# Attention units two to a row: logits of two units together, transposes and values by twos between projection steps

## The chip, the cores and the metric

One core of a Trainium2 chip. The metric is the device time of one execution in microseconds (us), median of three runs. The engines are TensorE (PE in the profile; its weight loads are PEld), VectorE (DVE), ScalarE (ACT), GpSimd (POOL) and SyncE (SP), which here issues most DMAs.

## The reference, cut to what matters

A two-layer decoder trunk on 512 tokens of width 1024, float32: a Mamba-2 mixer and a convolutional FFN, then a shared key and value projection, differential attention, and a second FFN. The change lies in the attention of layer 1, for each block `i` of 128 queries:

```python
logits = jnp.einsum('bqhcd,bkhcd->bhcqk', qblk, k).astype(jnp.float32) * scale
logits = logits + bias[None, :, None]
logits = jnp.where(dist >= 0, logits, -jnp.inf)
p = jax.nn.softmax(logits, axis=-1)
attn = p[:, :, 0] - lam * p[:, :, 1]
return jnp.einsum('bhqk,bkhd->bqhd', attn.astype(v.dtype), v)
```

There are 8 heads, each with two maps (`c`) of depth 64 and values of width 128. Queries and keys are RMS-normed per head and map; the result is RMS-normed per head, scaled and projected back.

## The kernel before, in words

Large products run as three matmuls on a high and a low part of both operands (float32r). A weight chunk (512 KB) comes by a DMA on SyncE's queue (L139), ScalarE writes its high part (L165, or L147 without a gain), VectorE the low part (L166, L151). Chunks are split two ahead of use.

The attention stage works with two kinds of PSUM banks, four each: `mm` for projections and `aux` for everything else.

- **Projections** (`proj`, L924 to L946): a generator. One `next` is a *step*: two token blocks by two rows of weights by three matmuls (L932 to L934), 12 matmuls of 512 columns. Four chunks of two steps make one projection. The order is: keys and queries of heads 0 to 3, then, as filling between attention units, values 0 (`v0`), keys and queries of heads 4 to 7 (`k1`, `q1`), values 1 (`v1`), and the output projection of heads 0 to 3 (`attn_out`, whose steps have 6 matmuls).
- **Behind a key or query projection** (`qk`, L948): ScalarE copies (L954) and squares (L955), VectorE sums (L956), a root follows (`rsqrt_act`: L434 VectorE, L435 and L436 ScalarE, L437 to L439 VectorE), VectorE multiplies each of four blocks (L963), and the blocks are transposed on TensorE (L970, four transposes for each, into an `aux` bank) and copied out by ScalarE (L971). The transposes are put between two steps of the projection that follows.
- **A unit** (`Unit`, L985) is a part of a head: query blocks (0, 1), or (2), or (3), so 24 units with 384, 384 and 512 key columns. It has four actions.
  - `logits`: with a head's first part, the head's bias row is fetched (L1000, SyncE) and turned (L1001, VectorE). TensorE forms the logits of both maps (L1014, depth 64, the two maps in the two halves of the array) in two `aux` banks; VectorE adds the bias, writes to SBUF and takes the maximum (L1020), negates it (L1023); ScalarE takes the exponential and its sum (L1028).
  - `weigh`: VectorE, reciprocal of the sums (L1035), factor (L1037), difference of the maps (L1041).
  - `turn`: TensorE transposes the result (L1049) into an `aux` bank, ScalarE copies it out (L1050).
  - `values`: TensorE multiplies by the values (L1060, `aux`), ScalarE scales (L1063).
- After a head's last part `normed_out` (L1066: ScalarE L1070, VectorE L1071, the root, VectorE L1073) and, some units later, `turned_out` (L1075: transposes L1079, ScalarE L1082, VectorE L1083).

TensorE's order in this stage is the program's order, since the stage is built with a manual schedule for TensorE; the instructions of the other engines are ordered by the scheduler. The main loop (L1148 to L1167) takes one unit a turn: at turn `t`, transposes of unit `t-2`, logits of `t`, weights of `t-1`, values of `t-3`, and then the number of steps that the list `steps` (L1144) gives, two for the first 13 turns. Tile buffers: three for the logits of each map, two for the transposed result, four for the reciprocals.

Of the kernel before, what the change touches and what calls it, by code (L numbers as in the profile page):

```python
# [39 lines left out]
def trunk_kernel(ctx: ExitStack, tc, x, ssm_ln_g, ssm_in_w, ssm_conv_w, ssm_conv_b, ssm_dt_bias,  # L40
# [19 lines left out]
    def aux_bank(name):  # L60
        return pp.tile([P, T], F32, tag="aux", name=name)
# [368 lines left out]
    def rsqrt_act(v, pl, name, shape, n):  # L430

        m = pl.tile(shape, F32, tag="rs_m", name="rsm_" + name, bufs=2)
        t = pl.tile(shape, F32, tag="rs_t", name="rst_" + name, bufs=2)
        dve.tensor_scalar(out=m, in0=v, scalar1=1.0 / n, scalar2=EPS, op0=ALU.mult, op1=ALU.add)  # L434
        act.activation(v, m, AF.Ln)  # L435
        act.activation(v, v, AF.Exp, scale=-0.5)  # L436
        dve.tensor_tensor(out=t, in0=v, in1=v, op=ALU.mult)  # L437
        dve.scalar_tensor_tensor(out=t, in0=t, scalar=-0.5, in1=m, op0=ALU.mult, op1=ALU.mult)
        dve.scalar_tensor_tensor(out=v, in0=t, scalar=1.5, in1=v, op0=ALU.add, op1=ALU.mult)  # L439
# [18 lines left out]
    def run(gen):  # L458
        for _ in gen:
            pass  # L460
# [19 lines left out]
    def chain(*gens):  # L480
        for g in gens:
            yield from g
# [417 lines left out]
    with tc.tile_pool(name="att_o", bufs=1) as op_, tc.tile_pool(name="att", bufs=1) as ap:  # L900
# [47 lines left out]
        def qk(key, dst, gcol, where):  # L948
            kn, ss = [], ap.tile([P, NT, 8], F32, tag="qss", name="ss" + key, bufs=2)

            def evac(b, ps, rt):
                t = ap.tile([P, T], F32, tag="kn", name="kn%s_%d" % (key, b), bufs=4)
                s = ap.tile([P, T], F32, tag="ksq", name="ksq%s_%d" % (key, b), bufs=1)
                act.activation(t, ps, AF.Copy, scale=rt[:, b:b + 1])  # L954
                act.activation(s, t, AF.Square)  # L955
                dve.reduce_sum(ss[:, b, :], s.rearrange("p (a q) -> p a q", a=8), axis=AX.X)  # L956
                kn.append(t)

            yield from proj(key, evac)
            rsqrt_act(ss, ap, key, [P, NT, 8], 64)  # L960
            for b in range(NT):
                v = kn[b].rearrange("p (a q) -> p a q", a=8)
                dve.tensor_tensor(out=v, in0=v, in1=ss[:, b, :].unsqueeze(2).to_broadcast([P, 8, 64]),  # L963
                                  op=ALU.mult)

            def turned(bs):
                for b in bs:
                    ps = aux_bank("kt%s_%d" % (key, b))
                    for h in range(4):
                        pe.transpose(ps[:, h * P:(h + 1) * P], kn[b][:, h * P:(h + 1) * P], ident)  # L970
                    act.activation(dst[:, :, b * P:(b + 1) * P], ps.rearrange("p (h t) -> p h t", h=4),  # L971
                                   AF.Copy, scale=c2[:, gcol:gcol + 1])

            for at, bs in zip(where, ((0, 1), (2, 3))):
                late.append((at, lambda bs=bs: turned(bs)))

        def vproj(key, i):
            def evac(b, ps, rt):
                act.activation(vt[b][:, i * 512:(i + 1) * 512], ps, AF.Copy, scale=rt[:, b:b + 1])
            yield from proj(key, evac)  # L980

        PARTS = ((0, 1), (2,), (3,))
        fl = lambda a: a.rearrange("p a b -> p (a b)")

        class Unit:  # L985
# [66 lines left out]
            def values(self):  # L1052
                h = self.h
                if self.part == 0:
                    self.st["ot"] = ap.tile([P, NT, P], F32, tag="ot", name="ot%d" % h, bufs=2)
                ps = aux_bank("po" + self.tag)
                for j, i in enumerate(self.ii):
                    o = self.off[j]
                    for k in range(i + 1):
                        pe.matmul(ps[:, j * P:(j + 1) * P], self.at[:, o + k * P:o + (k + 1) * P],  # L1060
                                  vt[k][:, h * P:(h + 1) * P], start=(k == 0), stop=(k == i))
                for j, i in enumerate(self.ii):
                    act.activation(self.st["ot"][:, i, :], ps[:, j * P:(j + 1) * P], AF.Copy,  # L1063
                                   scale=self.rc[:, j, 0:1])

        def normed_out(h, st):  # L1066
            ot = st["ot"]
            sq = ap.tile([P, T], F32, tag="ksq", name="osq%d" % h, bufs=1)
            so = ap.tile([P, NT], F32, tag="so", name="so%d" % h, bufs=2)
            act.activation(sq, fl(ot), AF.Square)  # L1070
            dve.reduce_sum(so, sq.rearrange("p (a q) -> p a q", a=NT), axis=AX.X)  # L1071
            rsqrt_act(so, ap, "o%d" % h, [P, NT], P)
            dve.tensor_tensor(out=ot, in0=ot, in1=so.unsqueeze(2).to_broadcast([P, NT, P]), op=ALU.mult)  # L1073

        def turned_out(h, st):  # L1075
            ot = st["ot"]
            ps = aux_bank("oT%d" % h)
            for i in range(NT):
                pe.transpose(ps[:, i * P:(i + 1) * P], ot[:, i, :], ident)  # L1079
            oh_ = op_.tile([P, T], F32R, tag="oh", name="oh%d" % h, bufs=6)  # L1080
            ol_ = op_.tile([P, T], F32R, tag="ol", name="ol%d" % h, bufs=6)
            act.activation(oh_, ps, AF.Copy, scale=c2[:, 50:51])  # L1082
            dve.scalar_tensor_tensor(out=ol_, in0=ps, scalar=c2[:, 50:51], in1=oh_.bitcast(F32),  # L1083
                                     op0=ALU.mult, op1=ALU.subtract)
            return oh_, ol_

        os = []

        def attn_out(i, norm, ms):

            pss, ws = {}, {}

            def part(m, k):
                if m not in pss:
                    if m % 2 == 0:
                        ws[m // 2] = chunk("ao%d_%d" % (i, m // 2))
                    pss[m] = mm_bank("ps_ao%d_%d" % (i, m))
                w = ws[m // 2]
                cols = slice(m % 2 * P, (m % 2 + 1) * P)
                mm3(pss[m], w[0][:, k, cols], w[1][:, k, cols], *os[4 * i + k], k == 0, k == 3)  # L1100
                if k == 3:
                    add_to_stream(m, pss[m], 24, norm)

            todo = [(m, k) for m in ms for k in range(4)]
            if ms[0] == 0:

                todo[:8] = [(m, k) for ks in (range(3), (3,)) for m in range(2) for k in ks]
            for n, mk in enumerate(todo):
                part(*mk)
                if n % 2:  # L1110
                    yield
# [21 lines left out]
        with tc.manual_schedule(engines={mybir.EngineType.PE}):  # L1133
            run(qk("k0", kT[0], 48, ((2, 1), (2, 3))))
            run(qk("q0", qT[0], 49, ((0, 3), (2, 1))))
            fill = chain(vproj("v0", 0), qk("k1", kT[1], 48, ((0, 3), (2, 3))), qk("q1", qT[1], 49, ((0, 3), (2, 1))), vproj("v1", 1),
                         attn_out(0, None, range(KB)))
            us = []
            for h in range(AH):
                st = {}  # L1140
                us += [Unit(h, part, st) for part in range(len(PARTS))]
            n = len(us)

            steps = [2] * 13 + [1, 1, 1] + [2, 1, 2, 1, 2, 1, 2] + [2, 1, 1, 1]  # L1144
            ots = []
            for _ in range(3):
                next(fill)
            for t in range(n + 3):  # L1148
                if 0 <= t - 2 < n:
                    us[t - 2].turn()  # L1150
                if t < n:
                    us[t].logits()
                    if t:
                        us[t - 1].weigh()
                elif t == n:
                    us[t - 1].weigh()
                if 0 <= t - 3 < n:
                    u = us[t - 3]
                    u.values()
                    if u.part == len(PARTS) - 1:  # L1160
                        normed_out(u.h, u.st)
                        ots.append([t + 1 + u.h // 4, u])
                for i in range(steps[t]):
                    next(fill)
                    if i == 0 and ots and ots[0][0] <= t and (steps[t] > 1 or t > n):
                        u = ots.pop(0)[1]
                        os.append(turned_out(u.h, u.st))  # L1167
            assert next(fill, None) is None
            last_out(norm1)

# [37 lines left out]
```

## Time and profile before

| what | us |
|---|---|
| median of three runs | 1356.53 (1356.06 to 1356.53) |
| span of the profiled execution | 1355.4 |
| attention stage, first logits to last values | about 802 to 963 |
| stretch 850 to 870: PE / DVE / ACT busy | 20.00 / 15.24 / 14.87 |
| stretch 910 to 930: PE / DVE / ACT busy | 20.00 / 15.31 / 14.78 |
| logits (L1014), 128 records | 801.7 to 952.6, median 0.43 each |
| transposes (L1049), 80 records | 814.7 to 959.6, median 0.27 each |

The profiled execution's span runs from the first to the last instruction; the time of a run also has what lies around the span, so the two differ by about 1 us. A float32 matmul leaves two records (two passes), a transpose one. Lengths of matmuls are modelled and overlap: the distance between starts is what counts. In the chain of waits each row is a start, the time until the next piece takes over, an engine, what it writes, the line and a count.

### The profile page before, as it was taken

What the parts mean: (1) busy time and instruction counts of PE and PEld (TensorE: products, weight loads), DVE (VectorE), ACT (ScalarE), POOL (GpSimd) and SP (SyncE); (2) the same over time, 40 slices, a digit from 0 to 9 for tenths busy, and PEclk for the clock granted to TensorE, in tenths of its full rate; (3) what the DMA queues carried; (4) which work ended last, traced back from release to release, by engine and by line L of the source; (5) the groups of instructions that cost most, each with busy time, mean ns of one, the idle gap of its engine ahead of it and who ended that gap; (6) DMA issues with size and microseconds to landing.
All of it is one profiled execution on the core that took longest, in us unless ns stands there. A gap on an engine that the chain in (4) does not pass through costs nothing.

```text
span 1355.4 us, 16857 instructions
## 1 busy us (share of the span) xinstructions
PE 1347.2 (99%) x6421; PEld 1096.1 (81%) x6421; DVE 911.1 (67%) x1525; ACT 654.0 (48%) x1066; POOL 95.7 (7%) x120
## 2 busy tenths in 40 slices
PE   9999999999999999999999999999999999999998
PEld 7877887887888888888888777777888888888887
DVE  4989878688777774267754555778777773367742
ACT  5696844642444442234433556767654442134420
POOL 6230301200020000000001000000110000000000
PEclk9999999999999999999999999999999999999999
DMA  7462432432333333333323422221223333333322
GB/s 203 138 170 78 149 109 94 148 94 69 95 94 93 94 96 105 94 94 94 101 78 108 127 80 86 78 75 37 78 87 89 104 94 94 93 104 99 94 94 78
DMA packets 179905, 135.06 MB, mean 100 GB/s; under 512 B 6509, under 2 KB 163633, under 8 KB 179825
## 3 DMA queue, kind: packets, MB, share of 16 engines
q1 hardware_dynamic: 174048, 120.84, 30.2%
q0 software_dynamic: 4496, 12.05, 2.9%
q8 instruction: 50, 0.82, 0.3%
q10 hardware_dynamic: 1280, 1.10, 0.2%
q14 instruction: 31, 0.25, 0.1%
HBM read 131.72 MB, written 2.25 MB: 99 GB/s over the span
## 4 chain that ended last, share of the span: by engine, by line
PE 94%; DVE 2%; ACT 1%; DMA 1%; issue 1%; POOL 0%; SPq 0%; DVEq 0%; POOLq 0%; ACTq 0%
PE ps_g L197 6%; PE ps_g L196 6%; PE ps_g L198 6%; PE ps_u L197 6%; PE ps_u L196 6%; PE ps_u L198 6%; PE ps_in L198 5%; PE ps_in L197 5%; PE ps_in L196 5%; PE ps_d L851 3%; PE ps_d L197 3%; PE ps_d L196 3%; PE ps_d L853 3%; PE ps_d L852 3%; PE ps_d L198 3%; PE ps_o L198 2%
## 5 line engine op out<-in xcount | busy, mean ns | idle before, releaser
L196 PE MATMUL ps_u<-xgh,wh_u 128*128 128x512 f32 x352 | 137.4, 390 | 0.0
L197 PE MATMUL ps_g<-xgl,wh_g 128*128 128x512 f32 x352 | 137.0, 389 | 0.0
L196 PE MATMUL ps_g<-xgh,wh_g 128*128 128x512 f32 x352 | 137.0, 389 | 0.0
L198 PE MATMUL ps_u<-xgh,wl_u 128*128 128x512 f32 x352 | 137.0, 389 | 0.0
L198 PE MATMUL ps_g<-xgh,wl_g 128*128 128x512 f32 x352 | 137.0, 389 | 0.0
L197 PE MATMUL ps_u<-xgl,wh_u 128*128 128x512 f32 x352 | 136.9, 389 | 0.0
L196 PE MATMUL ps_in<-xgh,wh_in 128*128 128x512 f32 x304 | 120.9, 398 | 0.0
L197 PE MATMUL ps_in<-xgl,wh_in 128*128 128x512 f32 x304 | 120.8, 397 | 0.0
L198 PE MATMUL ps_in<-xgh,wl_in 128*128 128x512 f32 x304 | 119.6, 393 | 0.0
L151 DVE TENSOR_TENSOR wl_d<-wr_d,wh_d 128x1024 fp32r<-128x1024 f32 (+1 forms) x46 | 54.2, 1178 | 96.9 <-ACT wh_d L147 96.7
L147 ACT ACTIVATE wh_d<-wr_d 128x1024 fp32r<-128x1024 f32 (+1 forms) x46 | 47.1, 1024 | 130.6 <-PE ps_d L853 62.4
L875 ACT ACTIVATE hh<-vg 128x512 fp32r<-128x512 f32 x44 | 27.8, 632 | 114.9 <-DVE vg L874 114.9
L823 DVE TENSOR_TENSOR uu<-ps_u,nr_f 128x512 f32<-128x512 f32 x44 | 30.4, 692 | 78.0 <-PE ps_u L198 77.8
L198 PEld LDWEIGHTS ps_g<-xgh,wl_g 128*128 128x128 f32 x352 | 66.1, 188 | 13.8
L197 PEld LDWEIGHTS ps_g<-xgl,wh_g 128*128 128x128 f32 x352 | 66.0, 187 | 13.9 <-DVE xgl L413 0.3
L197 PEld LDWEIGHTS ps_u<-xgl,wh_u 128*128 128x128 f32 x352 | 66.2, 188 | 13.5
L196 PEld LDWEIGHTS ps_g<-xgh,wh_g 128*128 128x128 f32 x352 | 66.1, 188 | 13.6
L196 PEld LDWEIGHTS ps_u<-xgh,wh_u 128*128 128x128 f32 x352 | 66.1, 188 | 13.7
L198 PEld LDWEIGHTS ps_u<-xgh,wl_u 128*128 128x128 f32 x352 | 66.0, 188 | 13.7
L147 ACT ACTIVATE wh_g<-wr_g 128x1024 fp32r<-128x1024 f32 x44 | 46.7, 1062 | 51.6 <-PE ps_u L197 32.2
L196 PE MATMUL ps_d<-hh,wh_d 128*128 128x512 f32 x176 | 68.5, 389 | 0.0
L197 PE MATMUL ps_d<-hl,wh_d 128*128 128x512 f32 x176 | 68.5, 389 | 0.0
(348 smaller groups left out, 3176.7 us busy)
## 6 DMA issues: line engine op xcount, KB each, us to landing
wr_g<-in_ffn_up_w_dram SPq DMA_DIRECT2D x44, 512.0 KB, 3.8
wr_u<-in_ffn_up_w_dram SPq DMA_DIRECT2D x44, 512.0 KB, 3.9
wr_d<-in_ffn_down_w_dram SPq DMA_DIRECT2D x42, 512.0 KB, 3.6
wr_in<-in_ssm_in_w_dram SPq DMA_DIRECT2D x40, 512.0 KB, 3.9
m<-cumd POOLq DMA_DIRECT2D x16, 512.0 KB, 4.0
wr_out<-in_ssm_out_w_dram SPq DMA_DIRECT2D x16, 512.0 KB, 3.5
wr_k<-in_kv_w_dram SPq DMA_DIRECT2D x8, 512.0 KB, 3.8
wr_q<-in_q_w_dram SPq DMA_DIRECT2D x8, 512.0 KB, 3.8
```

The lines of the kernel that those rows point to most:

```text
L147: return act.activation(self.wh[:, :self.n], self.raw[:, :self.n], AF.Copy)
L151: return eng.tensor_tensor(out=self.wl[:, :self.n], in0=self.raw[:, :self.n], in1=self.wh[:, :self.n].bitcast(F32), op=ALU.subtract)
L196: pe.matmul(ps, wh, xh, start=start, stop=False)
L197: pe.matmul(ps, wh, xl, start=False, stop=False)
L198: return pe.matmul(ps, wl, xh, start=False, stop=stop).ins
L823: dve.tensor_tensor(out=u, in0=ps, in1=r, op=ALU.mult)
L851: pe.matmul(pss[b], hh[k][:, ts], wh[:, k - k0, :], start=k == 0, stop=False)
L852: pe.matmul(pss[b], hh[k][:, ts], wl[:, k - k0, :], start=False, stop=False)
L853: pe.matmul(pss[b], hl[k][:, ts], wh[:, k - k0, :], start=False, stop=k == n - 1)
L875: act.activation(h, ga, AF.Copy)
```

## The change

For the first 14 units the loop goes by pairs. A turn of the pair loop has: transposes of the two units of the pair before; a step (and, if due, `turned_out`); values of those two units; a step; the logits of this pair, both units one behind the other; `weigh` of the first unit; a step; `weigh` of the second; a step. So a pair has four steps, where two units had two each, and its transposes come two steps behind its logits. From unit 14 on the loop is the earlier one with one unit a turn, and its list of steps for turns 14 on is written anew: before, turns 14 to 26 had 1, 1, then 2, 1, 2, 1, 2, 1, 2, then 2, 1, 1, 1; now 1, 1, then 2, 1, 1, 1, 2, 1, 2, then 2, 1, 1, 1. The values and the `turned_out` of a head are given the same turns as before, counted in units.

```diff
-            steps = [2] * 13 + [1, 1, 1] + [2, 1, 2, 1, 2, 1, 2] + [2, 1, 1, 1]
...
+            def values(t):
+                u = us[t]
+                u.values()
+                if u.part == len(PARTS) - 1:
+                    normed_out(u.h, u.st)
+                    ots.append([t + 4 + u.h // 4, u])
+
+            def out_of(t):
+                if ots and ots[0][0] <= t:
+                    u = ots.pop(0)[1]
+                    os.append(turned_out(u.h, u.st))
+
+            two = 14
+            for t in range(0, two, 2):
+                if t:
+                    us[t - 2].turn()
+                    us[t - 1].turn()
+                next(fill)
+                out_of(t + 1)
+                if t:
+                    values(t - 2)
+                    values(t - 1)
+                next(fill)
+                us[t].logits()
+                us[t + 1].logits()
+                us[t].weigh()
+                next(fill)
+                us[t + 1].weigh()
+                next(fill)
+
+            steps = [1, 1] + [2, 1, 1, 1, 2, 1, 2] + [2, 1, 1, 1]
+            for t in range(two, n + 3):
+                places = steps[t - two]
+                if t - 2 < n:
                     us[t - 2].turn()
                 if t < n:
                     us[t].logits()
...
+                if two < t <= n:
                     us[t - 1].weigh()
...
+                if two <= t - 1 and t - 3 < n:
+                    values(t - 3)
+                for i in range(places):
                     next(fill)
...
+                    if i == 0 and (places > 1 or t > n):
+                        out_of(t)
```

More of the change, by code (lines that the diff above doesn't have):

```diff
@@ L1147, in trunk_kernel @@
                 next(fill)
-            for t in range(n + 3):
-                if 0 <= t - 2 < n:
+            def values(t):
[29 more added lines that the diff above has]
+                if t - 2 < n:
                     us[t - 2].turn()
@@ L1152, in trunk_kernel @@
                     us[t].logits()
-                    if t:
-                        us[t - 1].weigh()
-                elif t == n:
+                if two < t <= n:
                     us[t - 1].weigh()
[L1157 to L1163, printed above, removed]
+                if two <= t - 1 and t - 3 < n:
+                    values(t - 3)
+                for i in range(places):
                     next(fill)
-                    if i == 0 and ots and ots[0][0] <= t and (steps[t] > 1 or t > n):
-                        u = ots.pop(0)[1]
-                        os.append(turned_out(u.h, u.st))
+                    if i == 0 and (places > 1 or t > n):
+                        out_of(t)
             assert next(fill, None) is None
```

## The prediction

> **What bounds the kernel now.** I read the page first, then the waits of TensorE over the attention stage (790 to 970 us), then the busy time by stretches.
>
> ```profile
> span 1355.4 us, 16857 instructions
> ...
> PE 1347.2 (99%) x6421; PEld 1096.1 (81%) x6421; DVE 911.1 (67%) x1525; ACT 654.0 (48%) x1066; POOL 95.7 (7%) x120
> ```
>
> ```profile
> PE at L1049 <- DVE lg L1041: 0.4, 1, 0.4
> PE ktq L970 <- DVE knq L963: 0.2, 1, 0.2
> PE po L1060 <- DVE ol L1083: 0.2, 1, 0.2
> ```
>
> ```profile
> 870.00:890.00 20.00, 20.00 (x108) 15.35 (x107) 14.64 (x46) 14.92 (x36) 0.00 (x0) 1.00 0.26 77
> ...
> 930.00:950.00 20.00, 19.49 (x108) 14.00 (x108) 17.37 (x63) 14.45 (x43) 0.00 (x0) 1.00 0.15 41
> ```
>
> TensorE is busy for 99% of the span, and in the whole stage it waits 0.8 us. In the stretches the columns after the length are PE, PEld, DVE, ACT, then POOL and the granted clock (1.00, full): the other engines have room, except in 930 to 950, where VectorE is busy 17.37 of 20 us and TensorE's short wait for L1041 falls. So the change can win only by making TensorE's own stream shorter, and it can lose by making TensorE wait. Both have to be priced.
>
> **Part 1: what TensorE saves.** Between projections (128 partitions deep) a unit now visits TensorE as transposes (L1049), logits (L1014: two 64-deep matmuls side by side), values (L1060). The chain of waits for 944 to 966 us shows what a visit of the 64-deep form costs (start, length):
>
> ```profile
> 946.87 0.85 PE lg L1014 x4
> 947.72 0.86 PE po L1060 x6
> ...
> 952.12 1.06 PE lg L1014 x4
> 953.18 1.09 PE po L1060 x8
> ...
> 957.04 0.33 PE at L1049 x3
> 957.37 0.67 PE po L1060 x6
> ...
> 962.35 0.89 PE po L1060 x8
> ```
>
> Leaving: six passes of values take 0.86 behind logits and 0.67 behind transposes, eight take 1.09 and 0.89. Leaving costs 0.19 to 0.20. Entering: 512 columns take 1.06, 384 take 0.85, so 128 columns are 0.21; four are 0.84 and the other 0.22 is the entry. A visit costs about 0.41 on top of its columns. The stage makes 24 visits, one for each unit; with the first 14 units by twos it makes 7 + 10 = 17. Saved: 7 x 0.41 = 2.9 us. Against it: transposes and values no longer lean on logits but hand over to projections directly, some 5 more returns. The trace doesn't show values entered from a projection; the nearest row is L1060 behind transposes, at its plain 0.67, so I take 0.03 a return (0 to 0.2, the cost of leaving logits), 0.15 in all. **Net -2.75 us** (bounds -2.9 to -1.9).
>
> The Trainium skill says on its page TensorEngine Tiling (Array Packing), Key Properties, that a change of the tiling mode drains TensorE. By that rule fewer visits save time; the 0.41 us agree in kind.
>
> **Part 2: what the pairs do to the softmax chain.** The cover goes. A unit's chain today, from the timeline (units 0 and 1, picked rows):
>
> ```profile
> 796.10 2.50 DVE L963 TENSOR_TENSOR knq<-knq,ssq 128x512 f32<-128x512 f32 x4
> ...
> 801.71 0.93 PE L1014 MATMUL lg<-kT,qT 64*128 64x128 f32 x8
> ...
> 802.67 0.29 DVE L1020 CUSTOM_DVE_ANT_0 lg<-lg,tb 128x128 f32<-128x128 f32 x1 [2.38 <-PE lg L1014]
> ...
> 804.10 0.40 ACT L1028 ACTIVATE lg<-lg,mx 128x128 f32<-128x128 f32 x1 [1.46 <-DVE mx L1023]
> ...
> 806.00 0.18 DVE L1035 RECIPROCAL rc<-sm 128x4 f32<-128x4 f32 x1 [1.94 <-ACT lg L1028]
> ...
> 806.48 0.35 DVE L1041 SCALAR_TENSOR_TENSOR lg<-lg,sm,lg 128x128 f32<-128x128 f32 x1
> ...
> 808.07 0.48 DVE L1041 SCALAR_TENSOR_TENSOR lg<-lg,sm,lg 128x256 f32<-128x256 f32 x1
> ...
> 810.47 0.62 ACT L1028 ACTIVATE lg<-lg,mx 128x384 f32<-128x384 f32 x1 [3.27 <-DVE mx L1023]
> ...
> 811.28 0.39 PE L932 MATMUL ps_v<-wh_v,xgh 128*128 128x512 f32 x1
> ...
> 811.82 0.17 DVE L1035 RECIPROCAL rc<-sm 128x2 f32<-128x2 f32 x1 [1.38 <-ACT lg L1028]
> ...
> 812.27 0.62 DVE L1041 SCALAR_TENSOR_TENSOR lg<-lg,sm,lg 128x384 f32<-128x384 f32 x1
> ...
> 814.00 0.39 PE L932 MATMUL ps_v<-wh_v,xgh 128*128 128x512 f32 x1
> ...
> 814.68 0.49 PE L1049 MATMUL at<-ident,lg 128*128 128x128 f32 x3
> ```
>
> Unit 0's weights are ready at 808.55 and transposed at 814.68: 6.1 us to spare, more than two projection steps. A step is the 12 matmuls from 811.28 to 814.00, 2.72 us. From the chain I read: reading unit 0's logits to the first exponential 1.4 (802.67 to 804.10); its exponentials 1.87 (804.10 to 806.00, less 0.03 of hand-over); from the sums to the weights 1.23 when nothing comes between (806.00, two small ones, 0.35 and 0.48 overlapping by 0.08). Unit 1 (384 columns): exponentials 1.32 (810.47 to 811.82, less 0.03), weights 1.07 (811.82 to 812.89). Back to back a VectorE instruction counts about 0.08 less than its own length (four L963 in 2.50).
>
> In the changed kernel two steps, 5.4 us, lie between a row of logits and its transposes. A quiet pair needs: 1.0 to the first read (801.71 to 802.67), 1.4 of reading, 1.87 + 1.32 of exponentials, 1.07 of weights and 0.2 of hand-overs, 6.8 us from the row's start. TensorE arrives at 1.5 (the row) + 0.2 + 5.4 + 0.33 (the first unit's transposes) = 7.4. So a quiet pair just fits: 0 to 0.6 us to spare, and for the two with the wide unit first I count 0.1 each. **+0.2 us.** Two pairs are not quiet, and there what is queued on VectorE decides. I go by the order of the built instructions, with these lengths besides:
>
> ```profile
> L1028 ACT ACTIVATE lg<-lg,mx 128x512 f32<-128x512 f32 x16 | 11.4, 717 | 3.0 <-DVE mx L1023 2.5
> ...
> L1020 DVE CUSTOM_DVE_ANT_0 lg<-lg,tb 128x512 f32<-128x512 f32 x16 | 10.5, 688 | 5.6 <-PE lg L1014 5.6
> ...
> L1020 DVE CUSTOM_DVE_ANT_0 lg<-lg,tb 128x384 f32<-128x384 f32 x16 | 8.4, 553 | 4.5 <-PE lg L1014 4.5
> ...
> L166 DVE SCALAR_TENSOR_TENSOR wl_v<-wr_v,c,wh_v 128x512 fp32r<-128x512 f32 x9 | 6.7, 748 | 1.7 <-ACT wh_v L165 1.7
> ...
> L1020 DVE CUSTOM_DVE_ANT_0 lg<-lg,tb 128x256 f32<-128x256 f32 x16 | 6.5, 419 | 0.0
> ...
> L1041 DVE SCALAR_TENSOR_TENSOR lg<-lg,sm,lg 128x512 f32<-128x512 f32 x8 | 6.0, 750 | 0.2
> ...
> L1073 DVE TENSOR_TENSOR ot<-ot,so 128x512 f32<-128x512 f32 x7 | 4.8, 687 | 0.1
> ```
>
> ```profile
> 857.91 0.87 PE ktk L970 x8
> ```
>
> *Units 6 and 7* (the second half of the keys). Behind their row come a step, key transposes 0 and 1 (0.43 each, L970), a step, and the units' own transposes. The row holds all four auxiliary PSUM banks; key transpose 1 takes the bank of unit 6's second map. VectorE's queue: small ones of two root chains first (first read at about 1.5 us from the row's start), then reads of 128 twice (0.21 each), L1073 (0.60), a read of 256 (0.35), **the four L963 of the keys (2.41)**, and only then the last read of unit 6 (0.35), small ones 0.3: 5.95 us. TensorE wants the bank at 1.7 + 2.72 + 0.43 = 4.85: **1.1 us** of waiting. Onward VectorE reads unit 7 (0.48), negates the maxima (0.1), unit 6's exponentials end at 8.5 and its weights at 9.75; TensorE, 1.1 late, arrives at 5.95 + 0.43 + 2.72 = 9.1: **0.65 us**. Unit 7's weights: 9.75 + 1.07 = 10.8, wanted at 10.1: **0.7 us**. Together 2.45.
>
> *Units 10 and 11* (the second half of the queries). VectorE: a reduction and small ones (first read at 1.75), reads of 384 twice (0.96), one of 512 (0.61), small ones (0.75), L1073 (0.60), L963 of query block 0 (0.69), handed over at 5.4; TensorE wants it at 1.9 + 2.72 = 4.65: **0.8 us**, and 0.15 for block 1. Then two L963, the last read of unit 11 (0.61) and a weight split (0.67) stand before its maxima, which are out at 8.6; exponentials 1.5, then sum, scale and L1041, 1.3: weights at 11.5. TensorE, 0.95 late, arrives at 10.4: **1.1 us**. Together 2.05.
>
> *After the pairs* the list of steps has one projection place fewer at t = 18 (2,1,1,1,2 for 2,1,2,1,2): 1.37 us less cover in the stretch where VectorE is busy 17.37 of 20. Laid the same way one turn waits 0.7 more and the next 0.2 less: **+0.5 us** (0 to 1.4). Each of these nine waits may also cost something when TensorE starts again. The trace has one such start:
>
> ```profile
> 936.65 0.30 PE at L1049
> 936.96 0.44 PE at L1049 x2
> ```
>
> Three transposes took 0.74 where three took 0.33 at 957.04. Between 0 and 0.41 a wait, then; I take 0.03, 0.3 for all, because in that row the second transpose waited once more for VectorE, for the second L1041 of its unit.
>
> What moves besides: the first row of logits comes two steps later, each head's bias row (L1000 on SyncE's queue, L1001 on VectorE) and the weight loads keep their number and size; no row of TensorE's waits names a DMA, so I count them at nothing. If a weight were late, the step behind it would show it.
>
> **Sum**: -2.75 + 0.2 + 2.45 + 2.05 + 0.5 + 0.3 = +2.75 us. The profiled execution spans 1355.4 us; the median of the runs, 1356.5, is 1.1 us above, the work around the span. Forecast **1359.3 us**, 0.2% slower.
>
> **Rivals.** *Faster*: the two crowded pairs don't wait. The mechanism is VectorE's lead: if it finishes the square sums and root chains of the head, and the L963, before the row of logits begins, nothing stands between the reads. It decides at about 2.5 us, the lag of the four L963; then only the 2.75 remain, less some 0.7 at the end: 1354.5. For it speaks that ScalarE, which feeds those chains, is busy only 14.92 of 20; against it the built order, in which L963 follows the first reads. *Dearer waits*: the quiet pairs, which I let fit within 0.6, miss by 0.5 each (five pairs, +2.5), for instance when a ScalarE eviction slips between exponentials: 1361.8. The Trainium skill, on the same page under PSUM Bottleneck, warns that tiling speeds TensorE and not the reading of PSUM, which may then bound; the 1.4 us that VectorE takes to read unit 0 beside 0.93 us of its matmuls agree, and by that rule this rival would be the likely one. *It doesn't do what it says*: if a row of two units still pays between them as for two visits, the 2.9 fall away: 1362.1.
>
> **How the numbers follow.** Forecast 0.75 (own range 1358.0 to 1360.8), faster rival 0.08, dearer waits 0.12, no saving 0.05. The range 1357.2 to 1362.0 takes in the bounds of part 1 and of the stretch after the pairs, and most of the cost of starting again, and leaves the faster rival and the last one out. About 0.2% (2.7 us) is what a measurement can tell from no change; the forecast stands on that edge, so it splits evenly between slower and within; of the faster rival, whose time is 0.15% below, I count 0.03 beyond the bound. Slower: 0.37 + 0.12 + 0.05 = 0.54; within: 0.38 + 0.05 = 0.43; faster: 0.03.
>
> **What would show it.** TensorE's waits should name L963 before L970 for both keys and queries, L1020 before L970 once, and L1041 before L1049 in those two pairs, 4 to 5 us in all; values entered from a projection should stay near 0.67; the sum of waits in the quiet pairs should be under 0.5. I am wrong if those two pairs run without waits, or if every pair waits.

## The result and the profile after

The changed kernel takes 1358.62 us (median of 18 runs, 1358.33 to 1359.58), the kernel before 1356.51 in the same sessions (18 runs, 1355.72 to 1357.35). The ratio is 1.0015, with a 95% interval of 1.0009 to 1.0021: 2.1 us slower. The top of the page of the changed kernel:

```profile
span 1357.2 us, 16854 instructions
...
PE 1346.0 (99%) x6421; PEld 1096.0 (81%) x6421; DVE 911.2 (67%) x1525; ACT 652.8 (48%) x1066; POOL 96.2 (7%) x120
```

TensorE is busy 1.2 us less than before (1347.2) in a span that is 1.8 us longer: its stream became shorter, and it waits more. Two instructions frame the attention stage in every variant: the first query transpose (L970) and the last transpose of a head's output (L1079). In the timeline of TensorE (start, length) they stand, first in the kernel before and then in the changed one, at

```profile
796.94 1.23 PE L970 MATMUL ktq<-ident,knq 128*128 128x128 f32 x8 [0.16 <-DVE knq L963]
...
968.58 0.60 PE L1079 MATMUL oT<-ident,ot 128*128 128x128 f32 x4
```

```profile
796.54 1.23 PE L970 MATMUL ktq<-ident,knq 128*128 128x128 f32 x8 [0.16 <-DVE knq L963]
...
970.40 0.60 PE L1079 MATMUL oT<-ident,ot 128*128 128x128 f32 x4
```

The stage takes 171.64 us before and 173.86 after, 2.22 us more. All of the difference lies in it; ahead of it this execution was 0.40 us early. I call this distance the stage time below. Who TensorE waits for in the changed kernel, 790 to 975 us (sum, times, longest):

```profile
PE at L1049 <- DVE lg L1041: 1.1, 2, 0.9
PE ktk L970 <- DVE mx L1020: 0.8, 1, 0.8
PE at L1049 <- ACT wh_q L165: 0.7, 1, 0.7
PE ktq L970 <- DVE knq L963: 0.5, 2, 0.4
PE at L1049 <- DVE mx L1023: 0.5, 1, 0.5
PE po L1060 <- DVE ol L1083: 0.2, 1, 0.2
```

3.8 us, where the three rows of before came to 0.8. (A wait costs some 0.17 us more than this view shows, since it begins when the last projection matmul ends, 0.39 after its start, and the next one would have started 0.23 after it.) Two of its rows name the wrong releaser. The row that names ScalarE's high part of a weight chunk (L165) means unit 7's softmax weights, by the timeline of VectorE:

```profile
862.35 0.62 DVE L1041 SCALAR_TENSOR_TENSOR lg<-lg,sm,lg 128x384 f32<-128x384 f32 x1
```

They end at 862.97 and the transposes start at 863.11, 0.14 later; the last L1041 of the chain below ends at 898.06 and its transposes start at 898.20, 0.14 later too. L165 merely ended between. The row that names the negated maxima (L1023) means the weights of unit 17:

```profile
933.57 0.75 DVE L1041 SCALAR_TENSOR_TENSOR lg<-lg,sm,lg 128x512 f32<-128x512 f32 x1
...
934.30 0.17 DVE L1023 TENSOR_SCALAR mx<-mx 128x4 f32<-128x4 f32 x1
...
934.46 0.63 PE L1049 MATMUL at<-ident,lg 128*128 128x128 f32 x4 [0.50 <-DVE mx L1023]
```

L1041 ends at 934.32 and the transposes, which read what it wrote, start 0.14 later again; L1023 ends at 934.47, when they have already started. The busy time by stretches says where (the first column after the length is TensorE):

```profile
850.00:870.00 20.00, 18.39 (x102) 14.37 (x101) 13.73 (x42) 12.39 (x34) 0.00 (x0) 1.00 0.17 54
870.00:890.00 20.00, 20.00 (x103) 15.02 (x102) 13.69 (x44) 13.48 (x35) 0.00 (x0) 1.00 0.26 85
890.00:910.00 20.00, 18.74 (x107) 14.85 (x106) 14.28 (x44) 11.73 (x28) 0.00 (x0) 1.00 0.23 74
...
930.00:950.00 20.00, 19.07 (x112) 13.21 (x111) 17.76 (x61) 14.55 (x41) 0.00 (x0) 1.00 0.08 28
```

TensorE is idle for 1.61 us around units 6 and 7, for 1.26 around units 10 and 11, for 0.93 after the pairs (0.51 there before), and not at all around units 8 and 9 between them. The chain of the changed kernel shows both sides, the shorter stream and the waits:

```profile
806.88 1.50 PE lg L1014 x12
...
817.49 1.34 PE po L1060 x12
821.57 1.72 PE lg L1014 x12
...
854.39 0.60 DVE ot L1073
855.10 0.34 DVE lg L1020
855.44 2.41 DVE knk L963 x4
857.85 0.33 DVE lg L1020
...
863.11 0.52 PE at L1049 x3
...
891.95 1.89 DVE knq L963 x3
893.84 0.60 DVE lg L1020
...
897.30 0.76 DVE lg L1041
898.20 0.63 PE at L1049 x4
...
913.87 1.06 PE lg L1014 x4
...
918.21 0.86 PE lg L1014 x8
919.07 0.86 PE po L1060 x6
...
921.75 0.85 PE lg L1014 x4
```

In the first three rows two units together: logits of 768 columns in 1.50, values of both in 1.34. In the last four rows one unit at a time: 0.86 and 0.85 for the same logits, and values behind logits in 0.86 each. An entry is saved (0.86 + 0.85 - 1.50 = 0.21; for the pair with 512 columns 1.06 + 0.86 - 1.72 = 0.20) and a leaving (two units' values 1.72 - 1.34 = 0.38, less 0.19 for leaving the pair's row). In the middle the four multiplications of the keys, 2.41 us, stand between two reads of unit 6's logits; a bank is held until the read behind them, and everything behind it is late (the 0.8 us at key transposes in the waits above). The queries' multiplications stand the same way ahead of the last read of unit 11.

### The profile page after: what moved, and what is told of

It reads as the page before. It is cut to its first block, busy times and chain, and to the rows that moved or that the text cites. A ratio compares the mean times of both kernels' runs of the same rounds, so it can differ in the third digit from the quotient of the medians.

```text
span 1357.2 us, 16854 instructions
## 1 busy us (share of the span) xinstructions
PE 1346.0 (99%) x6421; PEld 1096.0 (81%) x6421; DVE 911.2 (67%) x1525; ACT 652.8 (48%) x1066; POOL 96.2 (7%) x120
## 4 chain that ended last, share of the span: by engine, by line
PE 90%; ACT 4%; DVE 4%; issue 1%; DMA 1%; POOL 0%; SPq 0%; DVEq 0%; ACTq 0%
PE ps_g L197 6%; PE ps_g L198 6%; PE ps_g L196 6%; PE ps_u L197 6%; PE ps_u L198 6%; PE ps_u L196 6%; PE ps_in L197 5%; PE ps_in L198 5%; PE ps_in L196 5%; PE ps_d L852 3%; PE ps_d L197 3%; PE ps_d L198 3%; PE ps_d L853 3%; PE ps_d L851 3%; PE ps_d L196 3%; PE ps_o L198 2%
```

## The experiments

My theory: the pairs save what was worked out, about 0.39 us each, and the loss is made by the order of VectorE's queue, at the two pairs whose reads of logits share it with L963, and by the list of steps after the pairs. The rivals: a pair costs wherever it stands, because it has half the cover; fewer visits save nothing; the list of steps is the whole loss. In the table the difference of the medians, the ratio to the kernel before on the same chip with its 95% interval, and the difference of the stage time to 171.64, from the same two rows of each kernel.

| kernel | medians, us | ratio | stage, us |
|---|---|---|---|
| the changed kernel | +2.11 | 1.0015 [1.0009, 1.0021] | +2.22 |
| keys later | +0.84 | 1.0007 [0.9998, 1.0016] | +0.56 |
| queries later | +1.37 | 1.0011 [1.0002, 1.0020] | +1.24 |
| both later | -0.40 | 0.9997 [0.9988, 1.0006] | -0.27 |
| single units, new steps | +0.89 | 1.0006 [0.9997, 1.0015] | +0.63 |
| both later, six more visits | +2.35 | 1.0018 [1.0009, 1.0027] | +2.52 |
| changed, three steps of cover | +3.95 | 1.0030 [1.0018, 1.0042] | +3.84 |
| three quiet pairs, new steps | -0.44 | 0.9997 [0.9988, 1.0006] | -0.42 |
| three quiet pairs, old steps | -1.25 | 0.9991 [0.9983, 1.0000] | -1.02 |
| both later, three steps | +0.12 | 1.0001 [0.9992, 1.0010] | +0.17 |
| the same, steps and outputs moved | -1.13 | 0.9992 [0.9983, 1.0001] | -0.82 |

Each variant ran 11 times (three steps of cover 6 times), the kernel before 21 to 33 times beside it. An interval is about 1.2 us to either side, wider than many of these differences. The stage time, from one profiled execution of each kernel, agrees with the medians within 0.31 us in every row, and I lean on both together.

### The multiplications out of the way: keys, queries, both

```diff
-            for b in range(NT):
-                v = kn[b].rearrange("p (a q) -> p a q", a=8)
-                dve.tensor_tensor(out=v, ...)
+            def scaled_up():
+                for b, v in enumerate([t.rearrange("p (a q) -> p a q", a=8) for t in kn]):
+                    with tc.issue_after(state["weighed"]) if mul_at else ExitStack(): dve.tensor_tensor(out=v, ...)
+            late.append((mul_at, scaled_up)) if mul_at else scaled_up()
...
-qk("k1", kT[1], 48, ((0, 3), (2, 3)))
+qk("k1", kT[1], 48, ((4, 1),), (2, 3), (range(NT),))
...
-qk("q1", qT[1], 49, ((0, 3), (2, 1)))
+qk("q1", qT[1], 49, ((2, 3),), (2, 1), (range(NT),))
```

The first kernel has the keys' line alone, the second the queries', the third both; `state["weighed"]` is the last L1041 of the unit weighed before. The transposes of the blocks have to follow: all four of the keys now stand in one row, three steps behind the old place of the first two and one behind that of the others (the expectation says four), and those of the queries two steps and one. The runs don't separate the later multiplications from the later transposes.

> The keys' four multiplications (L963) are put behind the weights of unit 7 in VectorE's queue, and the four key transposes stand together four places later. Theory (VectorE's order makes the waits, and the pairs themselves save): the waits of units 6 and 7 fall from 2.4 to under 1 us, those of units 10 and 11 stay near 1.8; the time is 1.2 to 1.8 us below the changed kernel, +0.3 to +0.9 us against the kernel before. Rival (a pair is dear wherever it stands, the multiplications only happen to be in the queue): the waits stay near 2.4 in units 6 and 7, +2 us against before.

> The same for the queries: their four multiplications (L963) behind the weights of unit 11, the four query transposes together two places later; the keys as in the changed kernel. Theory: the 1.8 us of waits in units 10 and 11 fall to under 0.8, those of units 6 and 7 stay at 2.4; 0.8 to 1.4 us below the changed kernel, +0.7 to +1.3 us against before. Rival (pairs are dear wherever they stand): nothing is gained, +2 us.

> Both: the keys' and the queries' multiplications behind the weights, all pairs as they are. Theory: the two gains add, 2.2 to 2.8 us below the changed kernel, -0.7 to 0 us against before: what the seven pairs save (2.65) is then given back by the rest of the waits and the shorter list of steps. Rival (pairs dear wherever they stand): +1.5 us or more against before.

Busy times around units 6 and 7 and around units 10 and 11, with the keys later:

```profile
850.00:870.00 20.00, 19.42 (x109) 15.66 (x107) 14.36 (x43) 11.34 (x32) 0.00 (x0) 1.00 0.27 76
890.00:910.00 20.00, 19.09 (x108) 15.14 (x107) 13.22 (x41) 12.00 (x30) 0.00 (x0) 1.00 0.21 66
```

with the queries later (850 to 870 is at 18.39, as in the changed kernel):

```profile
890.00:910.00 20.00, 19.68 (x111) 15.81 (x110) 14.45 (x42) 12.54 (x32) 0.00 (x0) 1.00 0.24 73
```

and with both:

```profile
850.00:870.00 20.00, 19.41 (x109) 15.65 (x107) 14.39 (x43) 11.33 (x32) 0.00 (x0) 1.00 0.24 75
890.00:910.00 20.00, 20.00 (x113) 16.02 (x112) 14.35 (x44) 12.84 (x32) 0.00 (x0) 1.00 0.22 66
```

Each edit fills the stretch of its own pair: 18.39 becomes 19.42 for the keys and stays for the queries, 18.74 becomes 19.68 for the queries. Together they shorten the stage by 2.49 us, to 0.27 below before, so the order of VectorE's queue, with the places of the transposes that hang on it, makes most of the loss: 1.66 us are gone when the keys are moved, 0.98 when the queries are. That a pair is dear wherever it stands is out. Two details went beside what I expected: with the keys alone moved, units 10 and 11 wait less too (19.09 for 18.74), so not all of the 1.66 stands at units 6 and 7; and the queries' medians, +1.37, are just above the expected +1.3.

What is left around units 6 and 7 is 0.59 us. In the chain of that kernel L1073 (0.60) still stands between the reads of unit 6, and a read of unit 7 (0.47) ahead of unit 6's negated maxima; which of them makes the rest wasn't tried. The new place of the transposes isn't free either. The logits of units 8 and 9 stand right behind the four key transposes, and one of their weight loads waits 0.28 us for ScalarE to copy these out (L971):

```profile
870.20 2.12 PE lg L1014 x9
```

The changed kernel has 1.72 for the same columns of units 2 and 3 (this row counts nine of its twelve records, but lasts until the next projection starts, as that one does).

### The list of steps alone

```diff
-steps = [2] * 13 + [1, 1, 1] + [2, 1, 2, 1, 2, 1, 2] + [2, 1, 1, 1]
+steps = [2] * 14 + [1, 1] + [2, 1, 1, 1, 2, 1, 2] + [2, 1, 1, 1]
```

> The kernel before, one unit at a time, but with the list of steps that the changed kernel has from t = 14 on (one projection place fewer at t = 18, one more ahead). Theory: only the term after the pairs is left, +0.3 to +0.8 us against before, with waits in the last 40 us of the stage alone. Rival (the list of steps, not the pairs, is what the change costs): +1.5 us or more.

+0.63 in the stage, +0.89 in the medians, the latter just above the expected +0.8 and by itself not told from nothing (the interval takes in 1.0000). Its waits have one row that the kernel before doesn't have and the changed kernel has, in the last 40 us: the one that names L1023, 0.5 us, which is the wait for unit 17's weights as above. So the list has a price of its own, 0.6 us by the stage, and is not the whole loss.

### Six more visits

Ahead of the values of the first unit of each of the first six pairs the kernel with both later issues one 64-deep matmul, whose result the values overwrite.

```diff
 ps = aux_bank("po" + self.tag)
+extra and pe.matmul(ps[:, :P], qT[0][:64, 0, :P], kT[0][:64, 0, :P], start=True, stop=True)
```

> Both multiplications late, as in the kernel with the keys' and the queries' L963 behind the weights, plus six 64-deep matmuls of 128 columns, one ahead of the values of the first unit of each of the first six pairs; what they write is overwritten. Theory (a visit of the 64-deep form costs 0.41 us beside its columns): 6 x (0.21 + 0.41) = +3.7 us against that kernel, about +3.3 against before. Rival (a visit costs nothing, so fewer visits save nothing): 6 x 0.21 = +1.3 us against that kernel.

+2.75 against the kernel with both later (2.35 + 0.40; stage 2.79): between the theory's 3.7 and the rival's 1.3. The chain tells why. Here, with the extra matmul (it stands on the line of the bank, L1056):

```profile
818.43 0.42 PE po L1056 x2
818.85 1.53 PE po L1060 x12
```

and in the kernel with both later:

```profile
817.50 1.34 PE po L1060 x12
```

0.42 + 1.53 - 1.34 = 0.61 a visit: 0.21 for the 128 columns, as with the logits, and 0.40 for the visit. Six of them would be 3.7. The rest is hidden by the waits that were left: what the extra visits take, VectorE has more time for. With both later,

```profile
PE at L1049 <- DVE lg L1041: 0.8, 2, 0.6
```

and with the visits,

```profile
PE at L1049 <- DVE lg L1041: 0.2, 1, 0.2
```

0.6 us of waits are gone by the view, most of the 0.9 that is missing; by the distances between the projection matmuls it is 0.49 at the transposes of units 6 and 7, 0.19 at those of units 10 and 11 and 0.19 behind the query transposes, 0.87 in all. So a visit costs 0.40 and the saving is real; that visits are free is out. The expectation forgot that time added ahead of a wait comes off the wait.

### More cover, old order

The step between values and logits is moved behind the weights: three steps instead of two between a row of logits and its transposes.

```diff
                 values(t - 1)
-            next(fill)
             us[t].logits()
...
             us[t + 1].weigh()
-            next(fill)
+            next(fill); next(fill)
```

> The changed kernel with the projection step between values and logits moved behind the weights: three steps instead of two between a row of logits and its transposes. Theory (what TensorE waits for in the two crowded pairs is the block of L963 in VectorE's queue, and the key and query transposes follow it as closely as before): the waits for L963 and L1020 ahead of L970 grow to 2 us each and no time is gained, +2.5 to +3.7 us against before. Rival (the pairs' shorter cover alone is the cause): the waits go, -1 us or less against before.

It is the slowest of all, +3.95 us (stage +3.84), a little above what was expected. Its waits:

```profile
PE ktk L970 <- DVE knk L963: 1.7, 1, 1.7
PE ktq L970 <- DVE knq L963: 1.2, 2, 1.0
```

The waits for weights in the two crowded pairs are gone, and so is the one for L1020. The key and query transposes, which stand as many places behind the projection as before, now wait for their multiplications: the row of logits comes earlier, and the root chain that these need gets in line behind it, for the keys behind the row's exponentials on ScalarE, the last of which starts at 856.75:

```profile
857.35 0.21 ACT L435 ACTIVATE ssk<-rsm_k 128x32 f32<-128x32 f32 x1
...
858.94 2.50 DVE L963 TENSOR_TENSOR knk<-knk,ssk 128x512 f32<-128x512 f32 x4
```

In the changed kernel the same multiplications start at 855.44. But moved is not longer: all rows of TensorE's waits add up to 3.8 us, as in the changed kernel, and around the two pairs TensorE is busy about as much (18.39 and 18.74 there):

```profile
850.00:870.00 20.00, 18.26 (x102) 14.68 (x102) 13.66 (x43) 12.62 (x35) 0.00 (x0) 1.00 0.17 53
890.00:910.00 20.00, 18.98 (x107) 15.33 (x106) 13.02 (x46) 11.92 (x33) 0.00 (x0) 1.00 0.27 86
```

So the 1.6 us by which the stage is longer than the changed kernel's are not in these waits. They go with the other thing that the edit does: values now stand right ahead of logits. The logits of units 4 and 5 take 2.35 in the chain, where the kernel with both later has 1.70 for the same columns (last experiment), and weight loads of logits wait for ScalarE's eviction of the values:

```profile
834.04 2.35 PE lg L1014 x8
```

```profile
PEld lg L1014 <- ACT ot L1063: 1.5, 5, 0.4
```

By the distances between projection matmuls, the six rows of values and logits take 3.1 us more than the two apart in the changed kernel, the transposes of the crowded pairs 0.7 less, and the projections, interrupted less often, 0.7 less. More cover moves the waits of the crowded pairs and hardly shortens them; what it adds stands at the banks.

### Quiet pairs alone

Pairs for units 0 to 5, single units from there (`two = 6`); first with the changed kernel's steps at the end, then with those of before.

```diff
-two = 14
+two = 6
...
-steps = [1, 1] + [2, 1, 1, 1, 2, 1, 2] + [2, 1, 1, 1]
+steps = [2] * 8 + [1, 1] + [2, 1, 1, 1, 2, 1, 2] + [2, 1, 1, 1]
```

```diff
+steps = [2] * 7 + [1, 1, 1] + [2, 1, 2, 1, 2, 1, 2] + [2, 1, 1, 1]
```

> Pairs for the first six units alone (three quiet pairs), the rest one at a time; the list of steps is the changed kernel's from t = 14 on. Theory (quiet pairs cost no wait): 3 x 0.39 saved = -1.2, +0.6 for the list of steps: -0.8 to -0.3 us against before. Rival (every pair waits or saves nothing): +0.5 us or more.

> The same three quiet pairs, with the list of steps that the kernel before has from t = 16 on (the place is taken at t = 15). Theory: the 1.2 us of three visits fewer stay, -1.2 to -0.7 us against before, the fastest so far. Rival (every pair waits or saves nothing): 0 us or above.

-0.44 us, as expected, and -1.25, just past the expected -1.2 (the stage, -1.02, lies within); the steps' price shows again as the difference, 0.6 in the stage and 0.8 in the medians. With the old steps TensorE's waits are the same three rows as before, with the same times (0.4, 0.2 and 0.2 us).

Three pairs at 0.39 make 1.2, less a few returns. This version has the lowest median of all. It is clearly faster than the changed kernel; against the kernel before, 0.9991 with an interval that touches 1.0000, the gain of 0.1% is likely and not shown, the more so as it is the best of ten variants.

### Order and cover together

Both multiplications later and three steps of cover (the two edits above in one kernel); then the same with the outputs' transposes (L1079) two steps later and the place in the list taken at t = 15.

```diff
-                out_of(t + 1)
...
-                next(fill); next(fill)
+                next(fill); out_of(t + 1); next(fill)
...
-steps = [1, 1] + [2, 1, 1, 1, 2, 1, 2] + [2, 1, 1, 1]
+steps = [1,0,2,1,2,1,2,1,2] + [2, 1, 1, 1]
```

> The multiplications L963 of keys and queries behind the weights, and three projection steps instead of two between a row of logits and its transposes (the step between values and logits moved behind the weights). Theory (order first, cover second: once L963 is out of the way, the longer cover takes up the waits for L1041 that were left in units 6, 7, 10 and 11): -1.5 to -0.9 us against before, where two steps with the late multiplications gave -0.4 and three steps alone +3.9. Rival (three steps are dear in themselves, for instance because values now stand right ahead of logits and these wait for PSUM banks): +0.5 us or more against before.

> As the kernel with late multiplications and three steps, with two more edits: the transposes of a head's output (L1079) stand two places later, off the row of logits, and the list of steps takes its place from t = 15 instead of t = 18. Theory (what is left is these two waits, 0.7 us ahead of one row of logits and 0.6 us after the pairs): -2.8 to -2.0 us against before, the fastest. Rival (the saved visits are given back wherever the place is taken): -1.2 us or above, no better than three quiet pairs.

+0.12 and -1.13: both miss what my theory expected, by 1.3 us from its middle. The first lies between theory and rival, the second is what its rival allowed, no better than three quiet pairs. TensorE's waits show nothing of it; in the second they are nearly those of before (0.3, 0.2 and 0.2 us). The waits of its weight loads do:

```profile
PEld lg L1014 <- ACT ot L1063: 1.8, 6, 0.4
```

Values now stand right ahead of logits, and the logits' last two maps take the PSUM banks from which ScalarE is still evicting the values (L1063). The matmuls before it seem to last longer, so that no idle time of PE is counted. In the chain of that kernel, for units 4 and 5 and for units 10 and 11 (where the chain's row counts seven of the eight records),

```profile
834.86 2.36 PE lg L1014 x8
...
883.65 2.24 PE lg L1014 x7
```

where the kernel with both later and two steps has for units 10 and 11, which have the same columns,

```profile
885.84 1.70 PE lg L1014 x8
```

0.66 and 0.54 us more in two rows: 1.2 us, about the size of the miss. So the longer cover does take up the waits for weights, and pays for it at the banks: the rival of the first expectation was right about the place, and too dear about the price.

## Why the prediction was right

Forecast +2.75 us against the median, measured +2.11; in the stage +2.22. By its own terms:

- **What TensorE saves**, -2.75: by the chain an entry of 0.20 to 0.21 and a leaving of 0.19, 0.39 to 0.40 a pair, 2.8 for seven without the returns. Three quiet pairs alone gave 1.02 in the stage with the old steps and 1.05 with the new ones (0.42 + 0.63), so 0.34 to 0.35 a pair with the returns, 2.4 for seven. Values entered from a projection stayed at 0.67 a unit (1.34 for two), as forecast. The extra visits confirm the price from the other side, 0.40 each. The Trainium skill says on its page TensorEngine Tiling (Array Packing), Key Properties, that a change of the tiling mode drains TensorE. The runs agree in that going in and out costs 0.40 us here; that it is a drain, no row shows.
- **The quiet pairs**, +0.2: nothing. TensorE is busy 20.00 of 20 around units 8 and 9, and three of them alone gain what three visits cost. So the rival of dearer waits fell. The Trainium skill's warning on the same page, under PSUM Bottleneck, that the reading of PSUM may bound, doesn't set the time here: two steps cover the reading.
- **Units 6 and 7**, +2.45: about 2.4 by the lengths of the blocks between projections, where key transposes and the two units' own transposes take 1.06 and 1.32 longer than undisturbed (2.08 and 2.13 from the start of the last projection matmul ahead of them to the next one behind them, for 1.02 and 0.81); forecast were 1.1 and, for the two units, 0.65 + 0.7. The wait at key transposition 1 for the bank (L1020, 0.8 in the view) is as told, behind the L963 block of 2.41 us. Moving that block gave 1.66 back, a part of it at units 10 and 11; by the same lengths 0.8 stayed at the transposes of units 6 and 7.
- **Units 10 and 11**, +2.05: about 1.84 in the same way (0.75 at the first query transposes, 1.09 at the second and the units' own, where 0.95 and 1.1 were forecast). Moving the multiplications gave 0.98 back when the keys were left, and 0.83 more than the keys alone.
- **After the pairs**, +0.5: 0.63 in the stage by the list of steps alone.
- **Starting again**, +0.3 for nine waits: not seen as a term of its own.

The three costs that were seen, 2.4, 1.84 and 0.63, less the stage's 2.22 leave 2.65 as the saving; this is a remainder, which no row measures by itself. With the 2.4 of the quiet pairs the sum is +2.47, 0.25 above the stage. So the costs were put some 0.6 us too dear (quiet pairs 0.2, units 6 and 7 0.05, units 10 and 11 0.2, starting again 0.3, against 0.13 too little after the pairs) and the saving 0.1 to 0.35 too large. The mechanism held term by term; that the total came as near as it did owes a little to errors that offset each other.

One wait was named inexactly: key transposes wait for L1020 alone, not for L963 first, since 2.72 us of projection cover the first two multiplications. The wait after the pairs is for L1041, as forecast, though its row names the maxima. *It doesn't do what it says* fell with the visits. The *faster* rival, VectorE's lead, was priced at -2.0, with some 0.7 for the end already in it; its condition, nothing between the reads, was made by hand only in part, with both multiplications later, and that gave -0.4. L1073 still stands between the reads, 0.8 us by the lengths of the blocks stay at units 6 and 7, and the logits behind four transposes in a row take 0.40 longer; the rest of the difference is not assigned.

## What to carry to other kernels

Where two tiles of work are put together to save a switch, the saving is small and certain and counts once for each pair; what it costs depends on what else stands in the queue of the engine that frees their banks, so place the pairs where that queue is empty, and leave the others single. Before adding cover, look at what orders the queue: three steps instead of two left the waits of the crowded pairs nearly as long as they were and added a wait at the banks, while moving two blocks of four instructions, with the transposes that follow them, took the loss away. When a row of waits names a releaser that the waiting instruction doesn't read from, look in the timeline for the one that it does. A move that fills one wait can make another behind a different resource, which the idle time of the matmuls alone may not show: look at the waits of the weight loads as well.

## What the runs showed of the hardware

A 64-deep matmul of 128 columns between 128-deep ones cost 0.61 us, nearly three times the 0.21 of its columns. A wait for a PSUM bank ahead of logits stood at the weight load (1.8 us in six waits) and lengthened the chain's piece of logits from 1.70 to 2.36 us, while the view of TensorE's own waits had no row for it.
